# A hand-ordered start for a gated MLP whose up projection uses seven products for eight

## The chip, the cores and the metric

The kernel runs on one core of one Trainium2 chip. The metric is the device time of one execution in microseconds, the median of three runs. The engines are PE (matrix multiply; PEld is its weight load), ACT, DVE and POOL; SP issues the DMA transfers. Activations and weights are float32; for PE each is split into a rounded high part and a low remainder ("fp32r"), and a product is three matmuls: high by high, high by low, low by high.

## The reference

Two layers, 512 tokens, width 1024. Each layer is a token mixer, a cross-attention into 256 memory tokens and a gated MLP, each between an RMS norm before and one after, with a residual sum. The change lies in the MLP (the FFN):

```python
def conv_ffn(h, w_up, conv_w, conv_b, w_down):
    u = causal_dwconv(h @ w_up, conv_w, conv_b)     # width 3
    a, g = jnp.split(u, 2, axis=-1)
    return (jax.nn.gelu(g, approximate=True) * a) @ w_down
```

`w_up` is 1024 x 5632 and `w_down` 2816 x 1024, so the FFN has 22 pairs (j = 0 to 21) of a linear tile and a gate tile, each of 128 features by 512 tokens.

## The kernel before, in words

**Order of the work.** PE always runs in the order in which the program is written. On ACT, DVE, POOL and SP the framework's planner chooses the order, from its own costs and each instruction's dependences, except inside `tc.manual_schedule(engines=...)`: instructions written there keep, on the named engines, the order in which they are written among themselves. Side tasks (the norms) are generators that yield waiting times (the table `PACE`); `drain` runs them to their end, `run` runs a generator and lets side tasks in between.

**Before the FFN.** The output projection of the cross-attention ends tile by tile of 128 tokens (t = 0 to 3). For each, `Tail.consume` adds the residual, and a task `pre_norm` (L241) norms the tile, transposes it on PE (`to_feature`, L272, two halves), writes the high and low parts into `xn` (four B buffers) and copies the float32 values into a piece of the `Forms` object (L283), a T buffer of which there are three. Layer 0 computes four tiles of layer 1's keys (`fill_k`) before its FFN starts.

**The first two pairs.** `ffn` (L1019) computes j = 0 and 1 directly: `feat_halves` (L180) takes the four weight units over the first 256 tokens, calls `between` (here: drain the norm tasks), and takes them over the other 256. As each tile ends, `up_conv` does the convolution (first term on ACT, L1031, the two others on DVE, L1036), the Gelu on ACT (L1058) and the gating product on DVE (L1050). One accumulator bank (`pg`) is held per tile, four in all.

**The other twenty pairs.** `up_products` (L1075) computes each pair j from seven products of 12 matmuls of 256 columns instead of eight: blocks of the input by blocks of the weights, where some operands are sums. The input's sums (s1 to s4) are made by `Forms.add`: four DVE sums for tile 2 with tile 0, four for tile 3 with tile 1 (L310 to L313), and a split of each result (L99 on ACT, L100 on DVE) into the S buffers. The weights' sums (t12, t34) are made by `add_up`, four additions on POOL (L1106 to L1109). `high` (ACT, L1125) and `low` (DVE, L1131; POOL for kind "b") split the weights: "a" plain weights, "t" and "u" sums, "b" a plain half. Products 1, 2, 3 and 4 take the plain input (3 with s4 instead), 5, 6 and 7 take sums. Product 1 goes to a scratch bank (`e1s`, tag `pa`); ACT copies it into the left half of the linear bank (L1170 for j = 2, L1213 later), product 2 adds to that; product 6 adds to the scratch bank, and DVE adds the result of product 5 (copied by ACT, L1190) into the gate bank (L1203), to which product 3 adds; product 7 adds to the scratch bank; ACT copies it to the linear bank's right half (L1178), DVE adds it to the gate bank's (L1179), and product 4 adds to the linear bank's. Since these banks are started by copies, a 512-column matmul first marks each bank as written (in `first`, for j = 2 and 3). PE's order for j = 2 is: two marks, product 1, 5, 6, two marks and product 1 of j = 3, product 2, 3, 7. The hand order on ACT, DVE and POOL is entered just before `up_products`; the first two pairs' work on these engines is left to the planner.

**The down stage.** `down` (L1223) adds 22 steps of eight tiles (h = 1 in four `pa` banks, then h = 0 in four `pg` banks), three matmuls of 512 columns each per tile; steps 0 and 1 are split ahead (`down_tile`). The `pg` banks are those of the last two pairs.

Every matmul has the line L107, every transpose L111.

Of the kernel before, what the change touches and what calls it, by code (L numbers as in the profile page):

```python
# [23 lines left out]
NF = 22  # L24
# [14 lines left out]
def trunk_kernel(ctx: ExitStack, tc: tile.TileContext, x4, memt, w, gw, gains, mcw, fcw, gb,  # L39
# [201 lines left out]
    def pre_norm(t, g, xn, wait, forms=None):  # L241
        xt = xs[t]
        v = None
        xgs = []
        ss = [sumsq(xt[:, 512 * h:512 * h + 512]) for h in range(2)]
        for h in range(2):
            c = slice(512 * h, 512 * h + 512)
            v2 = sm(1, tag="v", bufs=8)
            if h == 0:
                DVE.tensor_scalar(v2, ss[h], 1.0 / D, EPS, ALU.mult, ALU.add)  # L250
            else:
                DVE.scalar_tensor_tensor(v2, ss[h], 1.0 / D, v, ALU.mult, ALU.add)
            v = v2
        r = rstd(v)
        for h in range(2):
            c = slice(512 * h, 512 * h + 512)
            xg = pp.tile([128, 512], F32, tag="xg", name=nm("xg"), bufs=PACE["xg"])
            DVE.scalar_tensor_tensor(xg, xt[:, c], r, g[h], ALU.mult, ALU.mult)  # L258
            xgs.append(xg)
        yield wait  # L260
        while forms and t == 3 and not forms.s:
            yield 0.2
        xf = forms.piece() if forms else None
        for h in range(2):
            to_feature(xgs[h], t, xn[h], xn[2 + h], xf[:, 4 * h:4 * h + 4, :] if forms else None)
            yield PACE["nh"]
        if forms:
            while not forms.free:
                yield 0.2
            forms.add(t, xf)  # L270

    def to_feature(src, t, hi, lo, f32=None):  # L272
        p = pa()
# [9 lines left out]
    class Forms:  # L283


        def __init__(self):
            self.es = ExitStack()
            self.pool = self.es.enter_context(tc.tile_pool(name=nm("forms"), bufs=1, reuse_waits="tile"))
            self.pool.tile([128, 8 * PAD_S], F32, name=nm("pad")) if PAD_S else None
            self.s = None  # L290
            self.free = True
            self.xf = {}

        def wide(self, dt):
            return self.pool.tile([128, 8, 256], dt, tag="S", name=nm("S"), bufs=4)

        def piece(self):
            return self.flat().rearrange("p (k t) -> p k t", k=8)
# [4 lines left out]
        def add(self, t, xf):  # L303
            self.xf[t] = xf
            if t < 2:
                return
            self.s = self.s or [self.wide(F32R) for _ in range(4)]
            a, b = self.xf[t - 2], xf
            a11, a12, a21, a22 = a[:, :4], a[:, 4:], b[:, :4], b[:, 4:]
            DVE.tensor_add(a22, a21, a22)  # L310
            DVE.tensor_sub(a21, a11, a21)
            DVE.tensor_sub(a11, a22, a11)
            DVE.tensor_sub(a12, a12, a11)  # L313
            c = slice(128 * (t - 2), 128 * (t - 2) + 128)
            for i, f in ((0, b), (2, a)):
                split(f, self.s[i][:, :, c], self.s[i + 1][:, :, c])

        def part(self, which):
            i, k = {"s3": (0, 0), "s1": (0, 4), "s2": (2, 0), "s4": (2, 4)}[which]
# [699 lines left out]
    def ffn(l, xn, pend, forms):  # L1019
        act = act_of(xn)  # L1020
        es = ExitStack()
        fp = es.enter_context(tc.tile_pool(name=nm("ffn"), bufs=1, reuse_waits="tile"))
        fcw_t = fp.tile([128, 44, 4], F32, tag="fcw", name=nm("fcw"))
        SP.dma_start(fcw_t, fcw[l])
        gtiles = []
        us = {}

        def conv_first(j, half, acc):
            m = 22 * half + j
            us[j, half] = u = fp.tile([128, 512], F32, tag=f"u{half}", name=nm("u"), bufs=2)  # L1030
            ACT.activation(u, acc, AF.Identity, bias=fcw_t[:, m, 3:4], scale=fcw_t[:, m, 2:3])  # L1031

        def conv_rest(j, half, acc):
            m, u = 22 * half + j, us[j, half]
            for q in range(1, 3):
                DVE.scalar_tensor_tensor(u[:, q:], acc[:, :512 - q], fcw_t[:, m, 2 - q:3 - q], u[:, q:],  # L1036
                                         ALU.mult, ALU.add)

        def gated(j, lin, gate):
            if j < 16:  # L1040
                if j % 4 == 0:
                    us["big"] = bt()
# [10 lines left out]
        def up_conv(j, half, acc):  # L1053
            conv_first(j, half, acc)
            conv_rest(j, half, acc)
            u = us[j, half]
            if half:
                ACT.activation(u, u, AF.Gelu_apprx_tanh)  # L1058
            if (j, 1 - half) in us:
                gated(j, us.pop((j, 0)), us.pop((j, 1)))  # L1060

        def up_done(j, half):
            return lambda acc: up_conv(j, half, acc)

        drain(pend[:2])
        run(feat_halves(l, [U_UP + i for i in range(4)], act, [up_done(i // 2, i % 2) for i in range(4)],
                        lambda: drain(pend)))
        order = ExitStack()
        order.enter_context(tc.manual_schedule(engines={
            mybir.EngineType.Activation, mybir.EngineType.DVE, mybir.EngineType.Pool}))  # L1070
        with tc.manual_schedule(engines={mybir.EngineType.SP}):
            ready = run(up_products(l, fp, xn, forms, us, conv_first, conv_rest, gated, gtiles))
        return es, order, gtiles, ready

    def up_products(l, fp, xn, forms, us, conv_first, conv_rest, gated, gtiles):  # L1075

# [75 lines left out]

        def first(j):
            e1s[j] = pa()[:, left]
            if j < j0 + 2:
                for o in total(j):
                    mm(o, ws[j, "a"][0][:, :128], xn[0][:, 0, :], start=True, stop=True)
            yield from product(e1s[j], j, 1, True)

        for j in (j0, j0 + 1):  # L1160
# [12 lines left out]
        ready = []  # L1173
        for j in range(j0, NF + 1):
            p, real = j - 1, j < NF
# [15 lines left out]
            if p >= j0:  # L1191
                conv_rest(p, 1, G)
                if p > j0:
                    gated(p - 1, us.pop((p - 1, 0)), total(p - 1)[1])
                yield from product(A[:, right], p, 4)
                conv_first(p, 0, A)
                ACT.activation(G, us.pop((p, 1)), AF.Gelu_apprx_tanh)
                conv_rest(p, 0, A)
            if not real:
                gated(p, us.pop((p, 0)), G)  # L1200
                return ready
            yield from product(e1s[j], j, 6)
            DVE.tensor_add(total(j)[1][:, left], e1s[j], p5s[j])  # L1203
            high(j + 1, "t")
            low(j + 1, "t")
            if j + 1 == NF:
                ready.append(down_tile(0))
            else:
                yield from first(j + 1)
            high(j + 2, "a")  # L1210
            low(j + 2, "a")
            if j + 1 < NF:
# [8 lines left out]
            yield from product(e1s[j], j, 7)  # L1221

    def down(l, forms, gtiles, consume, order, ready):  # L1223
        accs = [[pg() for _ in range(4)], [pa() for _ in range(4)]]
        held = []

        def step(k, gh_, gl_, wu, t, h):
# [4 lines left out]
        for k in range(NF):  # L1232
# [8 lines left out]
            if k < NF - HELD:  # L1241
                for h in (1, 0):
                    for t in range(4):
                        step(k, gh_, gl_, wu, t, h)
                        yield
            else:
                order.close()
                held.append((k, gh_, gl_, wu))
# [10 lines left out]
    for l in range(L):  # L1259
# [15 lines left out]
        def cross_done():  # L1275
            drain(tasks)
            es.close()
            tail.open()
            tail.forms.free = l > 0

        run(tok_gen(l, U_WO, act_of([o_t[0], o_t[1], o_t[2], o_t[3]]), (0, 1), tail.consume,
                    seq=early(PACE["ec"], cross_done, lambda u: drain(tasks[u:u + 1]))))
        xn = tail.xn
        if l == 0:
            run(fill_k(mem_tiles(lambda: tail.forms.wide(F32R)), 1, range(PACE["kf"][0])))
            tail.forms.free = True
        pend = tail.tasks
        tail.close()
        forms = tail.forms
# [88 lines left out]
```

## Time and profile before

| | us |
|---|---|
| median of 3 runs | 1570.26 |
| lowest and highest | 1569.21, 1571.17 |
| the profiled execution | 1572.73 |
| its span | 1571.0 |
| PE busy in it | 1546.8 (98%) |
| DVE, ACT, POOL busy | 1049.2, 891.1, 327.6 |
| mean granted clock | 0.998 |

The profile is of one execution. Layer 0's FFN starts about 453 us into the span (its direct tiles), its twenty other pairs run from 476 to 681; in layer 1 these are 1213, and 1238 to 1445. In timelines a row has its start, its length, the engine, the source line, the operation, output<-inputs by names, the shape, and in brackets the engine's idle time before it with what ended it. Instructions of one engine may overlap a little in the records, and matmuls always do, so PE's pace is read from one start to the next.

### The profile page before, as it was taken

The numbers are of one execution on the slowest core, as the hardware profiler recorded it, in microseconds if no ns is written. First come the engines' busy times: TensorE is split into PE (matmuls) and PEld (weight loads), VectorE is DVE, ScalarE is ACT, GpSimd is POOL, SyncE is SP. The second block draws the span as 40 slices with busy tenths as digits, with TensorE's granted clock in tenths as the row PEclk, the third lists the DMA queues.
The fourth block names the chain that finished last, engine by engine and source line by source line (L and its number), as shares of the span: only waits on it lengthen the run. The fifth ranks groups of instructions, "written<-read, shape, count | busy, mean of one in ns | idle before, by whom it ended". The sixth has DMA issues, their size and how long they took to land.

```text
span 1571.0 us, 24501 instructions
## 1 busy us (share of the span) xinstructions
PE 1546.8 (98%) x9480; PEld 1371.6 (87%) x9480; DVE 1049.2 (67%) x1808; ACT 891.1 (57%) x1578; POOL 327.6 (21%) x292
## 2 busy tenths in 40 slices
PE   7999999999999999999999999999999999999998
PEld 5788888997899999988887888889988899999886
DVE  5687656746597777763376876567566977787433
ACT  5677574545466666652256775745445666666321
POOL 0000110100025666600010001101000466663000
PEclk9999999999999999999999999999999999999999
DMA  5331244553242333333323312444511233332321
GB/s 177 129 95 63 92 133 156 159 172 106 68 137 95 108 108 104 100 121 103 111 88 114 95 62 90 135 156 155 165 63 46 93 106 108 108 118 81 126 104 55
DMA packets 55430, 173.13 MB, mean 110 GB/s; under 512 B 6801, under 2 KB 9617, under 8 KB 55314
## 3 DMA queue, kind: packets, MB, share of 16 engines
q1 hardware_dynamic: 55314, 171.57, 33.5%
q8 instruction: 74, 1.21, 0.3%
q14 instruction: 42, 0.34, 0.1%
HBM read 165.22 MB, written 6.33 MB: 109 GB/s over the span
## 4 chain that ended last, share of the span: by engine, by line
PE 82%; DVE 6%; DMA 4%; ACT 3%; issue 2%; POOL 2%; SPq 0%; POOLq 0%; DVEq 0%; ACTq 0%
PE pg L107 51%; PE pa L107 28%; DMA raw<-in_w_dram 3%; PE pa L111 3%; DVE wlo L100 1%; ACT whi L99 1%; DVE xg L258 1%; POOL sm L232 1%; ACT junk L237 1%; DVE x L371 1%; DMA raw<-in_memt_dram 1%; DVE wlo L1131 1%; DVE B L279 0%; DMA raw<-dv 0%; DVE S L100 0%
## 5 line engine op out<-in xcount | busy, mean ns | idle before, releaser
L107 PE MATMUL pg<-B,whi 128*128 128x256 f32 (+1 forms) x1800 | 420.4, 327 | 4.0 <-DVE u L1036 2.5
L100 DVE TENSOR_TENSOR wlo<-raw,whi 128x1024 fp32r<-128x1024 f32 x188 | 231.2, 1231 | 216.6 <-ACT whi L99 216.0
L99 ACT CAST whi<-raw 128x1024 fp32r<-128x1024 f32 x188 | 197.2, 1050 | 221.7 <-PE pg L107 140.1
L107 PEld LDWEIGHTS pg<-B,whi 128*128 128x128 f32 x1800 | 290.2, 189 | 23.2 <-ACT b L1125 2.3
L107 PE MATMUL pg<-whi,B 128*128 128x512 f32 x896 | 297.7, 399 | 0.0
L107 PE MATMUL pg<-B,wlo 128*128 128x256 f32 (+1 forms) x896 | 288.0, 321 | 0.0
L107 PEld LDWEIGHTS pg<-whi,B 128*128 128x128 f32 x896 | 168.5, 188 | 34.9 <-DVE B L100 1.3
L232 POOL TENSOR_TENSOR sm<-sm,mhalf 128x1 f32<-128x1 f32 x56 | 34.3, 612 | 719.9 <-DVE sm L357 543.9
L107 PEld LDWEIGHTS pg<-B,wlo 128*128 128x128 f32 x896 | 168.9, 189 | 13.5
L107 PE MATMUL pg<-wlo,B 128*128 128x512 f32 x448 | 175.3, 391 | 0.6 <-DVE sm L250 0.6
L107 PE MATMUL pa<-S,whi 128*128 128x256 f32 x960 | 175.5, 283 | 0.0
L1036 DVE SCALAR_TENSOR_TENSOR u<-pg,fcw,u 128x511 f32<-128x511 f32 (+1 forms) x176 | 131.4, 747 | 38.2 <-ACT u L1031 35.2
L107 PEld LDWEIGHTS pa<-S,whi 128*128 128x128 f32 x960 | 147.5, 189 | 0.0
L107 PE MATMUL pa<-S,wlo 128*128 128x256 f32 x480 | 135.2, 282 | 0.0
L1131 DVE TENSOR_TENSOR wlo<-T,whi 128x1024 fp32r<-128x1024 f32 x80 | 104.0, 1301 | 10.8 <-ACT whi L1125 10.8
L107 PE MATMUL pa<-whi,S 128*128 128x512 f32 x320 | 105.9, 390 | 0.0
L107 PE MATMUL pg<-whi,S 128*128 128x512 f32 x320 | 105.4, 390 | 0.0
L1125 ACT CAST whi<-T 128x1024 fp32r<-128x1024 f32 x80 | 83.5, 1044 | 33.7 <-PE pg L107 28.6
L1031 ACT ACTIVATE u<-pg,fcw 128x512 f32<-128x512 f32 x88 | 68.5, 778 | 57.8 <-PE pg L107 37.8
L107 PEld LDWEIGHTS pg<-wlo,B 128*128 128x128 f32 x448 | 84.7, 189 | 15.8 <-DVE wlo L100 1.0
L107 PEld LDWEIGHTS pa<-S,wlo 128*128 128x128 f32 x480 | 90.9, 189 | 0.0
L1131 POOL TENSOR_TENSOR b<-rg,b 128x512 fp32r<-128x512 f32 x40 | 51.8, 1294 | 144.2 <-ACT b L1125 144.2
(264 smaller groups left out, 2947.8 us busy)
## 6 DMA issues: line engine op xcount, KB each, us to landing
raw<-in_w_dram SPq DMA_DIRECT2D x228, 512.0 KB, 3.5
rg<-in_w_dram SPq DMA_DIRECT2D x40, 512.0 KB, 3.4
gain<-in_gains_dram SPq DMA_DIRECT2D x11, 512.0 KB, 4.4
raw<-in_memt_dram SPq DMA_DIRECT2D x20, 256.0 KB, 3.1
tb<-tb_d SPq DMA_DIRECT2D x16, 256.0 KB, 3.6
x<-in_x_dram SPq DMA_DIRECT2D x8, 256.0 KB, 5.5
e<-nmu_d SPq DMA_DIRECT2D x8, 256.0 KB, 3.7
dv<-vf SPq DMA_DIRECT2D x8, 256.0 KB, 4.0
```

The source lines that it names most:

```text
L99: ACT.copy(hi, src)
L100: DVE.tensor_sub(lo, src, hi.bitcast(F32))
L107: PE.matmul(o, lhs, rhs, **kw)
L111: PE.transpose(o, src, idn)
L232: POOL.tensor_tensor(r, v, mhalf[:, :1], ALU.pow)
L237: ACT.activation(junk[:, :src.shape[-1]], src, AF.Square, accum_out=s_)
L258: DVE.scalar_tensor_tensor(xg, xt[:, c], r, g[h], ALU.mult, ALU.mult)
L371: DVE.scalar_tensor_tensor(xs[t][:, cc], self.hg[hh, t], r, xs[t][:, cc], ALU.mult, ALU.add)
L1031: ACT.activation(u, acc, AF.Identity, bias=fcw_t[:, m, 3:4], scale=fcw_t[:, m, 2:3])
L1036: DVE.scalar_tensor_tensor(u[:, q:], acc[:, :512 - q], fcw_t[:, m, 2 - q:3 - q], u[:, q:], ALU.mult, ALU.add)
L1125: ACT.copy(ws[j, kind][0], source(j, kind))
L1131: sub(ws[j, kind][1], source(j, kind), ws[j, kind][0].bitcast(F32), ALU.subtract)
```

## The change

- `pre_norm` no longer waits for buffers; tile 3's piece is a B buffer (`late`), which the linear-by-gate products of j = 12 to 15 use later. `Forms.add` is cut into `sums(t, i)` (two DVE sums) and `halve(t, i)` (one split).
- The hand order of ACT, DVE, POOL and of SP's loads is entered in `between`, before the second half of the first two pairs. `up_products` then runs in five steps: one in `between`, one behind each of the four direct tiles. Convolutions, Gelus and gating of j = 0 and 1 stand in that order.
- PE's order for the first products becomes: product 1 of j = 2, mark, product 1 of j = 3, mark, product 2 of j = 2, then 5, 6, mark, product 2 of j = 3, 3, 7. The other mark of j = 3 stands before its product 6.
- At the end, the first tile of down step 0 (three matmuls, h = 1, t = 0) goes before product 4 of the last pair.

```diff
@@ pre_norm
-        while forms and t == 3 and not forms.s:
-            yield 0.2
-        xf = forms.piece() if forms else None
+        xf = forms.piece(t) if forms else None
...
-        if forms:
-            while not forms.free:
-                yield 0.2
-            forms.add(t, xf)
+        if forms and t == 2:
+            forms.sums(t, 0)
@@ Forms
+        def sums(self, t, i):
+            a, b = self.xf[t - 2], self.xf[t]
+            a11, a12, a21, a22 = a[:, :4], a[:, 4:], b[:, :4], b[:, 4:]
+            if i == 0:
+                DVE.tensor_add(a22, a21, a22)
+                DVE.tensor_sub(a21, a11, a21)
+            else:
+                DVE.tensor_sub(a11, a22, a11)
+                DVE.tensor_sub(a12, a12, a11)
+
+        def halve(self, t, i):
             self.s = self.s or [self.wide(F32R) for _ in range(4)]
...
+            split(self.xf[t - 2 * i], self.s[2 * i][:, :, c], self.s[2 * i + 1][:, :, c])
@@ ffn
+        def gelu(j):
+            ACT.activation(us[j, 1], us[j, 1], AF.Gelu_apprx_tanh)
...
+        def between():
+            drain(pend)
+            order.enter_context(tc.manual_schedule(engines={
+                mybir.EngineType.Activation, mybir.EngineType.DVE, mybir.EngineType.Pool}))
+            loads.enter_context(tc.manual_schedule(engines={mybir.EngineType.SP}))
+            next(up)
 
         def up_done(j, half):
-            return lambda acc: up_conv(j, half, acc)
+            def f(acc):
+                conv_first(j, half, acc)
+                conv_rest(j, half, acc)
+            return f
...
-                        lambda: drain(pend)))
+                        between, 4 * [lambda: next(up)]))
+        ready = run(up)
@@ up_products
-        sums = [pg() for _ in range(4)]
+        sums = []
...
         for j in (j0, j0 + 1):
             load_a(j)
             load_g(j)
+        forms.halve(2, 0)
+        forms.sums(2, 1)
+        high(j0, "a")
+        low(j0, "a")
+        forms.halve(2, 1)
         add_up(j0)
         load_a(j0 + 2)
-        for kind in "atu":
-            high(j0, kind)
-            low(j0, kind)
-        high(j0, "b")
-        yield from first(j0)
-        ACT.copy(total(j0)[0][:, left], e1s[j0])
+        yield
+        forms.sums(3, 0)
+        yield
         high(j0 + 1, "a")
         low(j0 + 1, "a")
+        forms.sums(3, 1)
+        forms.halve(3, 0)
+        forms.halve(3, 1)
+        high(j0, "t")
+        low(j0, "t")
+        gelu(0)
+        yield
+        high(j0, "b")
+        high(j0, "u")
+        low(j0, "u")
+        yield
+        gated(0, us.pop((0, 0)), us.pop((0, 1)))
+        gelu(1)
+        gated(1, us.pop((1, 0)), us.pop((1, 1)))
+        yield
+        banks = [pg() for _ in range(4)]
+        sums += [banks[i] for i in (0, 2, 1, 3)]
+        for j in (j0, j0 + 1):
+            yield from first(j)
+            A, G = total(j)
+            mark(A)
+            ACT.copy(A[:, left], e1s[j])
+        yield from product(total(j0)[0][:, left], j0, 2)
...
+                if not real:
+                    first_down = pa()
+                    gh_, gl_, wu = ready[0]
+                    mm3(first_down, gh_[:, :128], gl_[:, :128], wu[0][:, 512:], wu[1][:, 512:], True, False)
+                    yield
                 yield from product(A[:, right], p, 4)
...
+            if j == j0 + 1:
+                mark(total(j)[1])
             yield from product(e1s[j], j, 6)
+            if j == j0:
+                mark(total(j)[1])
             DVE.tensor_add(total(j)[1][:, left], e1s[j], p5s[j])
...
-            yield from product(total(j)[0][:, left], j, 2)
+            if j == j0:
+                yield from product(total(j + 1)[0][:, left], j + 1, 2)
+            elif j > j0 + 1:
+                yield from product(total(j)[0][:, left], j, 2)
```

## Rows read from the trace of the kernel before

**Rows 1.** The page's busy lines: engine, busy us, share, instructions.
```profile
PE 1546.8 (98%) x9480; PEld 1371.6 (87%) x9480; DVE 1049.2 (67%) x1808; ACT 891.1 (57%) x1578; POOL 327.6 (21%) x292
```
**Rows 2.** The chain of waits, layer 0's FFN: start, length, engine and line, count.
```profile
484.92 2.88 PE pg L107 x24
```
**Rows 3.** PE's timeline where layer 0's other pairs begin.
```profile
476.07 0.40 PE L107 MATMUL pg<-B,whi 128*128 128x512 f32 x1
477.00 0.48 PE L107 MATMUL pg<-B,whi 128*128 128x512 f32 x1 [0.53 <-DVE u L1036]
...
482.05 0.40 PE L107 MATMUL pa<-B,whi 128*128 128x256 f32 x2
483.45 0.39 PE L107 MATMUL pa<-B,wlo 128*128 128x256 f32 x1 [1.00 <-DVE wlo L1131]
```
**Rows 4.** PE's timeline where layer 1's other pairs begin.
```profile
1238.14 0.47 PE L107 MATMUL pg<-B,whi 128*128 128x512 f32 x1
1240.59 0.77 PE L107 MATMUL pg<-B,whi 128*128 128x512 f32 x1 [1.98 <-DVE u L1036]
1241.16 0.63 PE L107 MATMUL pa<-B,whi 128*128 128x256 f32 x2
...
1243.72 0.49 PE L107 MATMUL pa<-S,whi 128*128 128x256 f32 x2
...
1247.38 0.39 PE L107 MATMUL pa<-B,whi 128*128 128x256 f32 x2
1249.04 0.39 PE L107 MATMUL pa<-B,wlo 128*128 128x256 f32 x1 [1.26 <-DVE wlo L1131]
```
**Rows 5.** Windows: stretch, length, PE, PEld, DVE, ACT, POOL busy, granted clock, DMA.
```profile
1240.50:1243.90 3.40, 3.31 (x14) 3.24 (x15) 3.10 (x3) 2.84 (x4) 3.32 (x3) 0.50 0.61 212
...
1226.00:1238.00 12.00, 11.57 (x96) 11.18 (x94) 11.90 (x13) 6.62 (x8) 6.32 (x4) 1.00 0.01 2
```
**Rows 6.** PE's timeline between product 7 and product 4 of layer 0's last pair.
```profile
679.19 0.28 PE L107 MATMUL pa<-S,wlo 128*128 128x256 f32 x1
679.91 0.50 PE L107 MATMUL pg<-B,whi 128*128 128x256 f32 x2 [0.45 <-ACT pg L1178]
```
**Rows 7.** ACT's timeline, layer 0: table load, copy for j = 2, second Gelu.
```profile
476.93 1.28 ACT L1058 ACT_TABLE_LOAD   x1 [0.92 <-DVE u L1036]
...
479.43 0.37 ACT L1170 COPY pg<-pa 128x256 f32<-128x256 f32 x1
...
481.42 0.63 ACT L1058 ACTIVATE u<-u 128x512 f32<-128x512 f32 x1 [0.65 <-DVE u L1036]
```
**Rows 8.** Groups by shape, ACT, 484 to 660: count, busy us, mean ns, idle before.
```profile
L1125 ACT CAST whi<-T 128x1024 fp32r<-128x1024 f32 x35 | 36.6, 1045 | 14.8 <-PE pg L107 14.8
L1031 ACT ACTIVATE u<-pg,fcw 128x512 f32<-128x512 f32 x34 | 26.5, 778 | 25.2 <-PE pg L107 16.7 <-DVE pg L1179 8.5
...
L1213 ACT COPY pg<-pa 128x256 f32<-128x256 f32 x18 | 6.6, 369 | 0.7 <-PE pa L107 0.7
```
**Rows 9.** Groups by shape, DVE, 484 to 660.
```profile
L1036 DVE SCALAR_TENSOR_TENSOR u<-pg,fcw,u 128x511 f32<-128x511 f32 x34 | 25.4, 747 | 14.9 <-ACT u L1031 14.9
L1131 DVE TENSOR_TENSOR wlo<-raw,whi 128x1024 fp32r<-128x1024 f32 x18 | 21.8, 1212 | 0.0
```
**Rows 10.** DVE's and POOL's timelines, layer 0: one kind of sum twice, an addition.
```profile
453.60 0.69 DVE L311 TENSOR_TENSOR T<-T,T 128x512 f32<-128x512 f32 x1
...
463.20 1.68 DVE L311 TENSOR_TENSOR T<-T,T 128x512 f32<-128x512 f32 x1
...
461.61 2.72 POOL L1106 TENSOR_TENSOR T<-rg,raw 128x512 f32<-128x512 f32 x1 [14.66 <-DVE B L279]
```
**Rows 11.** DVE's timeline, layer 1: the last scaling before tile 3's transposes.
```profile
1220.42 1.42 DVE L258 SCALAR_TENSOR_TENSOR xg<-x,sm,gain 128x512 f32<-128x512 f32 x2
```
**Rows 12.** DVE's timeline, layer 0: the last pair's convolution and gating.
```profile
683.22 1.53 DVE L1036 SCALAR_TENSOR_TENSOR u<-pg,fcw,u 128x511 f32<-128x511 f32 x2
...
684.85 0.69 DVE L1050 TENSOR_TENSOR gt<-u,pg 128x512 f32<-128x512 f32 x1
```

More of the change, by code (lines that the diff above doesn't have):

```diff
@@ L290, in __init__, with piece @@
             self.s = None
-            self.free = True
             self.xf = {}
+            self.late = None
         def wide(self, dt):
             return self.pool.tile([128, 8, 256], dt, tag="S", name=nm("S"), bufs=4)
-        def piece(self):
-            return self.flat().rearrange("p (k t) -> p k t", k=8)
+        def piece(self, t):
+            if t == 3:
+                self.late = bt()
+            f = self.late.rearrange("p a b -> p (a b)")[:, :1024] if t == 3 else self.flat()
+            self.xf[t] = f.rearrange("p (k t) -> p k t", k=8)
+            return self.xf[t]
         def flat(self, dt=F32):
             return self.pool.tile([128, 1024], dt, tag="T", name=nm("T"), bufs=3)
[L303 to L306, printed above, removed]
-            self.s = self.s or [self.wide(F32R) for _ in range(4)]
[L308 to L313, printed above, removed]
+        def sums(self, t, i):
[8 more added lines that the diff above has]
+        def halve(self, t, i):
+            self.s = self.s or [self.wide(F32R) for _ in range(4)]
             c = slice(128 * (t - 2), 128 * (t - 2) + 128)
-            for i, f in ((0, b), (2, a)):
-                split(f, self.s[i][:, :, c], self.s[i + 1][:, :, c])
+            split(self.xf[t - 2 * i], self.s[2 * i][:, :, c], self.s[2 * i + 1][:, :, c])
         def part(self, which):
@@ L1041, in gated @@
                 if j % 4 == 0:
-                    us["big"] = bt()
+                    us["big"] = bt() if j < 12 else forms.late
                 gt = us["big"][:, j % 4, :]
@@ L1051, in gated, with up_products @@
             gtiles.append(gt)
[L1053 to L1060, printed above, removed]
+        def gelu(j):
+            ACT.activation(us[j, 1], us[j, 1], AF.Gelu_apprx_tanh)
+        order, loads = ExitStack(), ExitStack()
+        up = up_products(l, fp, xn, forms, us, conv_first, conv_rest, gelu, gated, gtiles)
+        def between():
[4 more added lines that the diff above has]
+            next(up)
         def up_done(j, half):
-            return lambda acc: up_conv(j, half, acc)
+            def f(acc):
+                conv_first(j, half, acc)
+                conv_rest(j, half, acc)
+            return f
         drain(pend[:2])
         run(feat_halves(l, [U_UP + i for i in range(4)], act, [up_done(i // 2, i % 2) for i in range(4)],
-                        lambda: drain(pend)))
[L1068 to L1072, printed above, removed]
+                        between, 4 * [lambda: next(up)]))
+        ready = run(up)
+        loads.close()
         return es, order, gtiles, ready
-    def up_products(l, fp, xn, forms, us, conv_first, conv_rest, gated, gtiles):
+    def up_products(l, fp, xn, forms, us, conv_first, conv_rest, gelu, gated, gtiles):
         j0 = 2
@@ L1154, in first, with mark @@
             e1s[j] = pa()[:, left]
-            if j < j0 + 2:
-                for o in total(j):
-                    mm(o, ws[j, "a"][0][:, :128], xn[0][:, 0, :], start=True, stop=True)
             yield from product(e1s[j], j, 1, True)
+        def mark(o):
+            mm(o, ws[j0, "a"][0][:, :128], xn[0][:, 0, :], start=True, stop=True)
         for j in (j0, j0 + 1):
@@ L1200, in up_products @@
                 gated(p, us.pop((p, 0)), G)
-                return ready
+                return ready, first_down
+            if j == j0 + 1:
+                mark(total(j)[1])
             yield from product(e1s[j], j, 6)
+            if j == j0:
+                mark(total(j)[1])
             DVE.tensor_add(total(j)[1][:, left], e1s[j], p5s[j])
@@ L1207, in up_products @@
                 ready.append(down_tile(0))
-            else:
+            elif j > j0:
                 yield from first(j + 1)
@@ L1211, in up_products @@
             low(j + 2, "a")
-            if j + 1 < NF:
+            if j0 < j < NF - 1:
                 ACT.copy(total(j + 1)[0][:, left], e1s[j + 1])
-            yield from product(total(j)[0][:, left], j, 2)
+            if j == j0:
+                yield from product(total(j + 1)[0][:, left], j + 1, 2)
+            elif j > j0 + 1:
+                yield from product(total(j)[0][:, left], j, 2)
             high(j + 1, "u")
@@ L1223, in down @@
     def down(l, forms, gtiles, consume, order, ready):
-        accs = [[pg() for _ in range(4)], [pa() for _ in range(4)]]
+        ready, first_down = ready
+        accs = [[pg() for _ in range(4)], [first_down] + [pa() for _ in range(3)]]
         held = []
@@ L1243, in down @@
                     for t in range(4):
-                        step(k, gh_, gl_, wu, t, h)
-                        yield
+                        if k or t or not h:
+                            step(k, gh_, gl_, wu, t, h)
+                            yield
             else:
@@ L1278, in cross_done @@
             tail.open()
-            tail.forms.free = l > 0
         run(tok_gen(l, U_WO, act_of([o_t[0], o_t[1], o_t[2], o_t[3]]), (0, 1), tail.consume,
@@ L1285, in trunk_kernel @@
             run(fill_k(mem_tiles(lambda: tail.forms.wide(F32R)), 1, range(PACE["kf"][0])))
-            tail.forms.free = True
         pend = tail.tasks
```

## The prediction

> **What bounds the kernel now.** I read the page's busy lines first: PE is busy 98% of the span [rows 1], so a change that leaves the number of matmuls alone can win or lose only where PE stands still. The chain of waits then gives PE's pace in the FFN: 24 matmuls of 256 columns in 2.88 us, 0.12 us each [rows 2]; one of 512 columns I count at 0.23, twice the columns. With that pace I went along PE's timeline around each FFN's start and end and took what is above it as lost. In layer 0 the second mark starts 0.93 after the first, 0.70 more than its 0.23, released by a DVE convolution; and the low part of j = 3's first weights comes 1.40 after two matmuls worth 0.24, a loss of 1.16 [rows 3]. Sum 1.86. In layer 1 the same places cost 2.45 - 0.23 = 2.22, then 0.57 - 0.23 = 0.34, then 1.66 - 0.24 = 1.42 [rows 4], sum 3.98. There the clock falls as well: the granted clock is 0.50, the 1.2 GHz level, in 1240.5 to 1243.9 [rows 5], and the 12 matmuls from 1241.16 take 2.56 instead of 1.44, a loss of 1.12 [rows 4]. Layer 1's start costs 5.1 in all. At the end of the up products PE stands 0.60 (0.72 less 0.12) until ACT has copied a left-hand sum [rows 6]; this stop stands once in each layer. Everything in reach is 1.86 + 5.1 + 1.2 = 8.2 us.
>
> The windows say why the start stalls: DVE is busy 11.90 of the 12.00 us in which the second half of layer 1's first four tiles runs [rows 5]. It is late with sums, splits and convolutions, and PE waits at whichever result it needs first.
>
> **Part by part.**
>
> *What is not changed in amount.* Seven products of 12 matmuls per j, four marks, eight sums, the splits: all the same number. Two products (first of j = 3, second of j = 2) go ahead of product 5. Until product 2 of j = 2 begins, PE now has two products and two marks, 24 x 0.12 + 2 x 0.23 = 3.34 us, that need no sum. `piece(3)` takes a B buffer in place of a T, and the up products later use it as their fourth big tile: no instruction more, nothing. The T buffers of tiles 0 and 2 come free before tile 3's sums, so POOL's four additions for j = 2 go earlier; PE waits for none of them today, nothing.
>
> *What the hand order puts in a row.* The order on ACT and DVE now begins before the second half of the first four tiles and holds the convolutions, both Gelus and the gating, which the planner placed freely. Product 2 of j = 2 adds onto a bank that ACT must first fill by its copy; the copy is written behind `gelu(1)`, and that needs the last direct tile's convolution. Today the copy runs ahead of that Gelu (479.43 against 481.42) [rows 7]. So PE, 3.34 us after its last direct tile, waits for this chain, counted from the end of the second direct tile, (0,1):
>
> first convolution term on ACT 0.78, the two others on DVE 2 x 0.75, low part of j = 3's "a" 1.21, sums(3,1) 2 x 0.69; cast of the last half 1.05, cast "t" 1.05, table load 1.28, Gelu 0.63, ACT term of tile (1,0) 0.78, DVE 2 x 0.75, low "u" 1.21, DVE 2 x 0.75 for tile (1,1), Gelu 0.63, copy 0.37 [rows 7 to 10]. That is 14.9; two DVE instructions of 0.75 span 1.42 [rows 9, 11], so neighbours on one engine overlap by 0.08, some 0.4 in the chain: 14.5. Up to the sums it is 4.8, behind them 9.7.
>
> *Layer 0.* The last direct tile ends at 476.07 [rows 3], so tile (0,1) ends 48 x 0.12 = 5.76 earlier, at 470.3. The copy is through at 484.8; PE arrives at 476.07 + 3.34 = 479.4. New stall 5.4, old 1.86: +3.5. A DVE with nothing else to do cannot shorten this, since sums(3,0) and sums(3,1) now stand behind the convolutions. Bounds, with 14.0 and 15.2 for the chain: +3.0 and +4.2.
>
> *Layer 1.* PE arrives at 1238.14 + 3.34 = 1241.5. By the chain from the end of tile (0,1), 1232.4 + 14.5, the copy is there at 1246.9. By DVE's load: it is free at 1221.84 [rows 11]; up to sums(3,1) stand eight sums and two feature splits of 0.69, four operations of 1.21 and four convolution terms of 0.75, 14.7, less 18 x 0.08: 1235.1. POOL's four additions fall into this, and a sum took 1.68 instead of 0.69 while POOL was adding [rows 10]; four such are 4.0, none is 0, I take the middle, 2: 1237.1 + 9.7 = 1246.8. Both say 1247, with 1246.5 and 1249 as bounds. New stall 5.5 (5.0 to 7.5), old 3.98: +1.5.
>
> *The clock.* A stop of 2.45 was followed by the 1.2 GHz level in layer 1 [rows 4, 5]; those of 0.93 and 1.40 in layer 0 cost the following matmuls nothing, which keep 0.12 [rows 2, 3]. Stops of 5.4 and 5.5 should bring it in both. I price each at the 1.1 that the rows show, between 0 and three times that: layer 0 +1.1, layer 1 1.1 - 1.1 = 0.
>
> *The three down matmuls.* 3 x 0.23 = 0.68 fills the stop of 0.60: product 4 begins at 679.19 + 0.12 + 0.68 = 679.99 [rows 6], as before, ends at 681.43, and the down stage starts 0.68 ahead. Five of its tiles later, at 684.83, PE reaches the bank of A(21), one more on, at 685.51, that of G(21); DVE frees them at 684.75 and 685.54 [rows 12], plus some 0.1 of handing over: 0.15 is given back. Gain 0.55 per layer (0 to 0.7): -1.1.
>
> *j = 3's product 3* follows its product 6 by 12 matmuls instead of 24, 1.44 us for a DVE add that stands behind a convolution. Counted from product 4's end the add is through after 0.78 + 1.42 + 0.42 and two handings over, about 3.0, and product 3 arrives at 0.23 + 24 x 0.12 = 3.1: nothing, at worst 0.3.
>
> Sum: layer 0 +3.5 + 1.1, layer 1 +1.5 + 0, down -1.1: **+5.0 us**. The profiled execution took 1572.73 (span 1571.0), 2.5 above the median 1570.26; the difference is carried over to the median: 1575.3.
>
> On the step that decides, the trace shows ACT idle 14.8 us in all before 35 "whi<-T" casts that wait for PE, with later work queued behind them [rows 8]; that nothing ever passes it does not prove. The Trainium skill, "TensorE: Matmul & The Clock Gate" (Architectural detail: the array is 16x 32x32), says that the queues of ACT and DVE are strictly first in, first out. By it the copy cannot pass a waiting Gelu, and the two stalls stand; were it not so, rival A would hold.
>
> **The rivals.**
>
> *A, faster: the copy is not late.* If the copy is taken before `gelu(1)`, 3.34 us of new cover meet the old waits: 1.86 in layer 0 and 5.1 in layer 1 go, and the down gain comes on top: -8.1, 1562.2. For it: low "t" and the halves, which product 5 needs, are ready three DVE operations after sums(3,1), at about 478.7 and 1240.8, just when PE would arrive. Against: rows 7 show the free order only because the planner placed the Gelu. It decides at a copy done by 479.4 and 1241.5.
>
> *B, no change: the chain holds, but the clock stays up* in both layers: 3.5 + 1.5 - 1.1 (layer 1's old loss) - 1.1 = +2.8, and +1.9 with the lower bounds of the stalls: 1572.2 to 1573.1. For: layer 0's stops cost no clock. Against: 5.4 is over twice the stop that did.
>
> *C, much slower: the hand order starts late.* If in layer 0 DVE does not take tile 0's and 2's halves while the first half runs, 11 of its 13 us before sums(3,1)'s end begin only at 476.07 - 96 x 0.12 = 464.5: 464.5 + 11 + 2 + 9.7 = 487.2, 2.4 later; with the clock's upper bound, 2.2 more in each layer, 1577.7 to 1582.1. For: all these operations are written behind `between`. Against: DVE ran layer 0's sums(2) at 453.6, well ahead of that point [rows 10].
>
> **How the numbers follow.** Forecast 60%, A 14%, B 16%, C 10%. The forecast's own range: stalls -1.0 to +2.7, clock up to +4.4, down +1.1 around +5.0; the ends rarely meet, so 1573 to 1579.5. The whole range leaves out most of A and C's upper end: 1567.0 to 1580.5. A difference under 0.2%, 3.1 us, cannot be told from no change here. The forecast is slower by more than that in about nine of ten, C always, the lower half of B and a tenth of the forecast are no change: slower 0.68, same 0.18, faster 0.14.
>
> **What would show it.** PE's timeline has one long stop in each FFN's start, between a mark and a "pg<-B" matmul of 256 columns, released by ACT's copy that fills the bank; ahead of it ACT's rows run table load, Gelu, term, two casts, term, Gelu, copy. Its length, 5.4 and 5.5, tests the chain; a granted clock of 0.50 behind it in both layers, with matmuls of 0.21, tests the price. The 0.60 stop before product 4 is gone. No long stop, or a copy ahead of the second Gelu, would make the forecast wrong.

## The result and the profile after

The changed kernel takes 1580.35 us (median; 1579.50 to 1581.21) against 1570.72 of the kernel before in the same comparison, a ratio of 1.0063 with a 95% interval of 1.0050 to 1.0076: slower by 9.6. I had forecast slower by 5.0, and no more than 1580.5. The profiled execution took 1581.21, span 1579.4. PE's work is what it was [rows 1]:

```profile
PE 1547.1 (98%) x9480; PEld 1371.6 (87%) x9480; DVE 1052.8 (67%) x1808; ACT 892.2 (56%) x1578; POOL 331.2 (21%) x292
```

I numbered the matmuls of both traces and subtracted the start of the n-th before from the n-th after. The difference is -0.3 ahead of layer 0's other pairs, +5.8 once they have begun, +3.95 at their end, +3.4 after the first down products; +9.0 once layer 1's pairs have begun, +8.5 at the end (1581.21 - 1572.73). So four places matter: the two starts (+6.15, +5.5), layer 0's pairs (-1.9), the down stages (-0.5 each).

PE's timeline after, layer 0's start, where [rows 3] had two short stops:

```profile
478.82 0.39 PE L107 MATMUL pg<-B,whi 128*128 128x512 f32 x1
485.13 0.80 PE L107 MATMUL pg<-B,whi 128*128 128x256 f32 x2 [5.91 <-ACT pg L1200]
485.72 0.41 PE L107 MATMUL pg<-B,wlo 128*128 128x256 f32 x1
485.94 0.63 PE L107 MATMUL pg<-B,whi 128*128 128x256 f32 x2
```

and layer 1's, where [rows 4] had three:

```profile
1244.09 0.40 PE L107 MATMUL pg<-B,whi 128*128 128x512 f32 x1
1253.52 0.79 PE L107 MATMUL pg<-B,whi 128*128 128x256 f32 x2 [9.02 <-ACT pg L1200]
```

One stop in each layer: 6.31 - 0.23 = 6.08 and 9.43 - 0.23 = 9.20 us. Both stand between the second mark and product 2 of j = 2 and end with ACT's copy into the bank, L1200. Behind each the clock is at the 1.2 GHz level; windows of that stretch, columns as in [rows 5]:

```profile
483.30:490.10 6.80, 4.97 (x23) 4.97 (x24) 4.06 (x3) 1.17 (x3) 5.15 (x4) 0.50 0.23 73
1247.90:1258.10 10.20, 4.58 (x21) 4.59 (x22) 7.58 (x7) 3.49 (x7) 8.16 (x5) 0.50 0.20 56
```

PE is busy only from the end of the stop on: 23 matmuls in 4.97 instead of 23 x 0.119 = 2.74, 21 in 4.58 instead of 2.50. The price is 2.2 and 2.1. Before, the clock fell in layer 1 alone, 1.12 by [rows 4]; e7 shows that this cost nothing in the end.

ACT's timeline after, layer 0, is the chain of the forecast in its order, against [rows 7]:

```profile
475.08 1.05 ACT L99 CAST S<-T 128x1024 fp32r<-128x1024 f32 x1 [2.18 <-DVE T L311]
476.04 1.04 ACT L1129 CAST whi<-T 128x1024 fp32r<-128x1024 f32 x1
477.10 1.28 ACT L1054 ACT_TABLE_LOAD   x1
478.40 0.63 ACT L1054 ACTIVATE u<-u 128x512 f32<-128x512 f32 x1
...
481.05 0.78 ACT L1031 ACTIVATE u<-pg,fcw 128x512 f32<-128x512 f32 x1
484.18 0.63 ACT L1054 ACTIVATE u<-u 128x512 f32<-128x512 f32 x1 [2.35 <-DVE u L1036]
484.71 0.63 ACT L1200 COPY pg<-pa 128x256 f32<-128x256 f32 x2
```

ACT is idle for 2.35 in front of the second Gelu while both copies, whose products ended by 479.1, wait behind it.

DVE's timeline after, layer 1, with POOL's beside it; compare the pairs of rows in [rows 10]:

```profile
1227.74 1.23 DVE L100 TENSOR_TENSOR S<-T,S 128x1024 fp32r<-128x1024 f32 x1 [1.11 <-ACT S L99]
...
1230.68 1.56 DVE L311 TENSOR_TENSOR T<-T 128x512 f32<-128x512 f32 x1
1232.16 2.33 DVE L1135 TENSOR_TENSOR wlo<-raw,whi 128x1024 fp32r<-128x1024 f32 x1
...
1235.55 1.52 DVE L1036 SCALAR_TENSOR_TENSOR u<-pg,fcw,u 128x511 f32<-128x511 f32 x2
1236.99 1.83 DVE L307 TENSOR_TENSOR B<-B 128x512 f32<-128x512 f32 x1
...
1242.76 0.69 DVE L311 TENSOR_TENSOR T<-T 128x512 f32<-128x512 f32 x1
```

```profile
1230.38 1.31 POOL L1110 TENSOR_TENSOR T<-rg,raw 128x512 f32<-128x512 f32 x1 [6.54 <-ACT B L277]
1231.77 1.63 POOL L1111 TENSOR_TENSOR T<-rg,T 128x512 f32<-128x512 f32 x1
1235.71 1.32 POOL L1112 TENSOR_TENSOR T<-rg 128x512 f32<-128x512 f32 x1 [2.30 <-DVE S L100]
1236.99 1.29 POOL L1113 TENSOR_TENSOR T<-raw,T 128x512 f32<-128x512 f32 x1
```

Three DVE instructions beside POOL's additions are stretched: 1.56 for 0.69, 2.33 for 1.21, 1.83 for 0.69, together 3.1. The convolution terms at 1235.55, which read a `pg` bank, run beside the third addition in their usual 1.52. The Trainium skill, "SBUF — State Buffer" (Who interferes with whom), says that a DVE instruction with two inputs in SBUF contends with a GpSimd (POOL) instruction that reads SBUF, and that one with at most one such input, outside DVE's 2-port modes, does not; these rows agree. Such stretches stand in the kernel before as well: in layer 1, at 1229.61, 1231.32 and 1235.44, DVE took 1.68, 1.68 and 1.90 for 0.69, 0.69 and 1.22. So the contention is not new with the change. sums(3,1), the last row of the first fence, ends at 1243.45.

The three down matmuls stand in the old stop of [rows 6]; PE's timeline after:

```profile
683.27 0.40 PE L107 MATMUL pa<-whi,T 128*128 128x512 f32 x1
683.50 0.40 PE L107 MATMUL pa<-wlo,T 128*128 128x512 f32 x1
683.74 0.39 PE L107 MATMUL pa<-whi,T 128*128 128x512 f32 x1
683.97 0.42 PE L107 MATMUL pg<-B,whi 128*128 128x256 f32 x2
```

### The profile page after: what moved, and what is told of

The parts are those of the page before. It is cut to its first block, busy times and chain, and to the rows that moved or that the text cites. A ratio compares the mean times of both kernels' runs of the same rounds, so it can differ in the third digit from the quotient of the medians.

```text
span 1579.4 us, 24488 instructions
## 1 busy us (share of the span) xinstructions
PE 1547.1 (98%) x9480; PEld 1371.6 (87%) x9480; DVE 1052.8 (67%) x1808; ACT 892.2 (56%) x1578; POOL 331.2 (21%) x292
## 3 DMA queue, kind: packets, MB, share of 16 engines
q8 instruction: 74, 1.21, 0.3%
HBM read 165.22 MB, written 6.33 MB: 109 GB/s over the span
## 5 line engine op out<-in xcount | busy, mean ns | idle before, releaser
L107 PE MATMUL pg<-B,whi 128*128 128x256 f32 (+1 forms) x1800 | 421.1, 327 | 15.0 <-ACT pg L1200 14.9
L1135 DVE TENSOR_TENSOR wlo<-T,whi 128x1024 fp32r<-128x1024 f32 x80 | 107.8, 1347 | 5.0 <-ACT whi L1129 5.0
L1135 POOL TENSOR_TENSOR b<-rg,b 128x512 fp32r<-128x512 f32 x40 | 55.4, 1385 | 155.0 <-ACT b L1129 155.0
```

Of the source, the lines that this page charges most:

```text
L107: PE.matmul(o, lhs, rhs, **kw)
L1135: sub(ws[j, kind][1], source(j, kind), ws[j, kind][0].bitcast(F32), ALU.subtract)
```

## Experiments

The theory: the stops come from the place of the two copies in ACT's hand order. The rivals: the new order of PE's products itself; the load on DVE and POOL; the clock; something in the other pairs. Each version is the changed kernel with one edit, unless said otherwise. A ratio is to the kernel before in the same comparison; its median lay between 1569.92 and 1571.01 there, so differences of about 1 between versions say nothing.

For some versions I also give the length of the two starts in the trace: from the first matmul of the second half of the first four tiles to the 346th behind it, idle ones not counted. It is 49.90 and 53.55 in the changed kernel (layers 0 and 1), 43.83 and 48.05 in the first execution of the kernel before, 43.73 and 48.39 in e7.

**e1: the second Gelu and the gating behind the copies.**

```diff
-        gated(0, us.pop((0, 0)), us.pop((0, 1)))
-        gelu(1)
-        gated(1, us.pop((1, 0)), us.pop((1, 1)))
...
             ACT.copy(A[:, left], e1s[j])
+        gated(0, us.pop((0, 0)), us.pop((0, 1)))
+        gelu(1)
+        gated(1, us.pop((1, 0)), us.pop((1, 1)))
```

> One edit of the changed kernel: gating of j = 0, the second Gelu and gating of j = 1 are written behind ACT's two bank copies instead of ahead of them. Theory 1 (the stop is ACT's copy standing in the chain behind the second Gelu): the copy now stands directly behind the last direct tile's ACT term, which in the changed kernel ran at 481.05 and 1249.44; it is through about 1.2 later, so PE goes on near 482.4 and 1250.8, the stops are 3.3 and 6.5 instead of 6.1 and 9.2, with a fall of the clock behind each as now; about 5.4 us less than the changed kernel, near 1575. Theory 2 (DVE's backlog holds PE wherever the copy stands: PE would stop as long at product 5): no gain, within 1 us of 1580.4.

Measured: 1574.07, ratio 1.0026 (1.0014 to 1.0037). PE's timeline, the ends of the two stops:

```profile
481.23 0.51 PE L107 MATMUL pg<-B,whi 128*128 128x256 f32 x2 [2.95 <-ACT pg L1197]
...
1245.46 0.79 PE L107 MATMUL pg<-B,whi 128*128 128x256 f32 x2 [5.94 <-ACT pg L1197]
```

The stops are 3.11 and 6.10, shorter by 3.0 and 3.1, and in this execution the clock falls in layer 1 alone; one new stop of 0.66 comes before product 3 of j = 3. The place of three lines is worth 1580.35 - 1574.07 = 6.3. The rest of the loss, over 3 us, stays; in ACT's timeline the copies now run right behind the last direct tile's term (480.13 and 480.80 in layer 0).

**e2: PE's new order kept, the hand order entered only behind the four direct tiles** (as before; the planner places the convolutions, Gelus and gating).

```diff
         def between():
             drain(pend)
-            order.enter_context(tc.manual_schedule(engines={
...
-            loads.enter_context(tc.manual_schedule(engines={mybir.EngineType.SP}))
             next(up)
...
+        order.enter_context(tc.manual_schedule(engines={
...
+        loads.enter_context(tc.manual_schedule(engines={mybir.EngineType.SP}))
         ready = run(up)
```

> The changed kernel's matmul order, its buffers and the down matmuls, but the hand order is entered only behind the four direct tiles, as in the kernel before; the planner orders ACT, DVE and POOL until then. Theory 1 (the hand order costs, PE's new order is free or gains): ACT copies the banks ahead of the second Gelu, the long stops go, and what is left are short waits for product 5's operands: at or under the kernel before, 1562 to 1571. Theory 2 (PE's new order itself costs, since product 2 needs a copy that product 5 did not): stops of 3 us or more stay before product 2, and the time stays over 1573.

Measured: 1569.65, ratio 0.9991 (0.9981 to 1.0002). ACT's timeline, layer 0:

```profile
478.73 0.63 ACT L1054 ACTIVATE u<-u 128x512 f32<-128x512 f32 x1
479.27 0.76 ACT L1031 ACTIVATE u<-pg,fcw 128x512 f32<-128x512 f32 x1
479.93 0.37 ACT L1200 COPY pg<-pa 128x256 f32<-128x256 f32 x1
483.21 0.63 ACT L1054 ACTIVATE u<-u 128x512 f32<-128x512 f32 x1 [2.91 <-DVE u L1036]
```

The first copy runs ahead of the second Gelu, as in [rows 7]; PE's stops before product 2 are 2.00 and 2.63, and the clock falls behind both. So the loss comes with the early hand order (of SP's loads too). PE's new order, together with the down matmuls, can't be told from the kernel before in time. In the trace it is no gain either: the starts take 45.13 and 48.47, 1.4 and 0.1 more than in e7, and each down stage gives back 0.5.

**e3: the kernel before with the three down matmuls moved** (in `up_products`, before product 4 of the last pair; `down` skips that tile).

```diff
+                if not real:
+                    first_down = pa()
+                    gh_, gl_, wu = ready[0]
+                    mm3(first_down, gh_[:, :128], gl_[:, :128], wu[0][:, 512:], wu[1][:, 512:], True, False)
+                    yield
```

> The kernel before with the first tile of down step 0 moved before product 4 of the last pair, and nothing else. Theory 1: the 0.60 stop before product 4 is filled in each layer and some 0.5 of it is kept: 1.0 us less than the kernel before (1569.7), with a trace in which PE is 0.5 ahead behind each FFN's end. Rival: the bank of the linear half is freed too late and all of it is given back: 0. For the second question, PE's pace of 0.1200 in layer 0's pairs before against 0.1187 in the changed kernel: if it belongs to the program's buffers, layer 0's pairs here run at 0.1200 as before.

Measured: 1570.00, ratio 0.9999 (0.9989 to 1.0008). The 0.6 stops are gone; in time a gain of 1 can't be told from none here.

**e4: idle matmuls in the stops**, 46 in layer 0, 72 in layer 1, into a scratch bank, so that PE does not stand.

```diff
+        idle = pa()
+        for _ in range((46, 72)[l]):
+            mm(idle[:, left], ws[j0, "a"][0][:, :128], xn[0][:, 0, left], start=True, stop=True)
         yield from product(total(j0)[0][:, left], j0, 2)
```

> The changed kernel with matmuls that need nothing and whose result is not used, 46 of 256 columns in layer 0 and 72 in layer 1, ahead of product 2 of j = 2, where PE stands 6.1 and 9.2 us. ACT's copy is as late as before; PE is busy until 0.6 us ahead of it. Theory 1 (the clock's fall behind each stop costs PE some 2.4 us per layer): the granted clock stays at 1.00 through both starts and the time is 4.5 to 5 us under the changed kernel's, 1575.5. Rival (behind the stop PE is held by DVE and ACT anyway): the clock stays up and the time does not change by 1 us. On the pace: if layer 0's faster pace in the changed kernel, 0.1187 against 0.1200, comes with the fall of the clock, its pairs run at 0.1200 here and 1.9 us of the gain are missing (1577.4).

Measured: 1576.11, ratio 1.0040 (1.0025 to 1.0055). The windows around the ends of the stops, as long as those of the changed kernel above:

```profile
483.50:490.30 6.80, 6.74 (x56) 6.70 (x57) 4.22 (x5) 3.22 (x6) 3.50 (x3) 1.00 0.24 78
1249.70:1259.90 10.20, 10.20 (x85) 10.15 (x86) 6.54 (x7) 4.87 (x8) 5.29 (x5) 1.00 0.18 54
```

The clock stays up and product 2 begins as long after the mark as it did (6.33 against 6.31 in layer 0): 1580.35 - 1576.11 = 4.2 is the price of the clock alone. The starts in the trace say the same, 47.71 and 51.55: 2.2 and 2.0 less.

**e5: without POOL's four additions for j = 2**; that pair's sums of weights are left out, and its t and u weights are values that are there already.

```diff
-            if j < NF:
+            if j == j0:
+                ts[j] = [forms.xf[t].rearrange("p k t -> p (k t)") for t in (0, 2)]
+            elif j < NF:
```

> The changed kernel without POOL's four additions for j = 2: its "t" and "u" are split from the float32 pieces of tiles 0 and 2 instead, so pair j = 2 is computed from other data; all else stands. Theory 1 (in layer 1 DVE's own backlog, stretched by POOL's additions, moves the chain): three of DVE's operations that took 1.56, 2.33 and 1.83 there take 0.69, 1.21 and 0.69, DVE is through sums(3,1) 3 us earlier, and layer 1's stop goes from 9.2 to 6.5 +- 0.5 (the chain from the second direct tile's end, 15.0 in layer 0, lets no more than 3.3 go); layer 0's stays at 6.1. Rival (handing over between ACT and DVE sets both stops): 9.2 stays within 1.

Measured, one run: 1577.45. PE's timeline at the ends of the two stops, then DVE's, the three instructions of layer 1 that POOL had stretched:

```profile
484.03 0.80 PE L107 MATMUL pg<-B,whi 128*128 128x256 f32 x2 [5.91 <-ACT pg L1202]
...
1249.77 0.79 PE L107 MATMUL pg<-B,whi 128*128 128x256 f32 x2 [5.97 <-ACT pg L1202]
```

```profile
1229.99 0.68 DVE L311 TENSOR_TENSOR T<-T 128x512 f32<-128x512 f32 x1
1230.59 1.22 DVE L1137 TENSOR_TENSOR wlo<-raw,whi 128x1024 fp32r<-128x1024 f32 x1
...
1234.38 0.68 DVE L307 TENSOR_TENSOR B<-B 128x512 f32<-128x512 f32 x1
```

Layer 0's stop is unchanged (6.07), layer 1's is 6.14 instead of 9.20: the 3.1 that layer 1 loses more than layer 0 is POOL's additions stretching DVE.

**e6: all of the Gelus, the gating and the splits of "b" and "u" behind the copies**.

```diff
-        gelu(0)
...
-        high(j0, "b")
-        high(j0, "u")
-        low(j0, "u")
...
-        gated(0, us.pop((0, 0)), us.pop((0, 1)))
-        gelu(1)
-        gated(1, us.pop((1, 0)), us.pop((1, 1)))
...
             ACT.copy(A[:, left], e1s[j])
+        gelu(0)
+        high(j0, "b")
+        high(j0, "u")
+        low(j0, "u")
+        gated(0, us.pop((0, 0)), us.pop((0, 1)))
+        gelu(1)
+        gated(1, us.pop((1, 0)), us.pop((1, 1)))
```

> The changed kernel with all that the two bank copies do not need written behind them: both Gelus, the splits "b" and "u" of j = 2, and the gating. ACT then has "t" of j = 2, the two direct tiles' terms, the copies. Theory 1: in layer 0 the copy is through at 478.9, when PE arrives (479.05): a stop under 0.3. In layer 1 it is 1.8 behind the "t" cast's end: a stop near 3.1 instead of 9.2, with a clock fall (2 us). 12 us and layer 0's 2.2 for the clock less than the changed kernel: 1566 +- 1.5, under both kernels. Rival (product 5 and what follows wait for the "u" split and the table load that now come later): stops of 3 us turn up behind product 2, and the time is over 1570.

Measured: 1573.89, ratio 1.0027 (1.0011 to 1.0043); 1566 was missed, and the rival's condition held. PE's timeline, its long waits:

```profile
487.51 2.93 PE L107 MATMUL pg<-S,b 128*128 128x256 f32 x12 [3.18 <-DVE pg L1241]
...
1243.40 0.51 PE L107 MATMUL pg<-B,whi 128*128 128x256 f32 x2 [2.70 <-ACT pg L1193]
...
1252.35 1.86 PE L107 MATMUL pg<-S,b 128*128 128x256 f32 x7 [2.75 <-DVE pg L1241]
```

The copy's stop is gone in layer 0 and 2.86 in layer 1, but product 3 now waits 3.34 and 2.91 for the DVE add into the gate bank. DVE's timeline, layer 0:

```profile
482.27 1.47 DVE L1135 TENSOR_TENSOR wlo<-T,whi 128x1024 fp32r<-128x1024 f32 x1 [1.69 <-ACT whi L1129]
483.66 3.45 DVE L1050 TENSOR_TENSOR B<-u,u 128x512 f32<-128x512 f32 x2
487.04 0.42 DVE L1241 TENSOR_TENSOR pg<-pa,p 128x256 f32<-128x256 f32 x1
```

The add stands behind both gating products, which take 3.45 while POOL adds.

**e7: the kernel before once more**, unchanged.

> The kernel before, unchanged, profiled once more. In its first profile PE's pace in layer 0's twenty pairs was 0.1200 us per matmul, in every other kernel's and in layer 1 0.1187. If the pace changes from one execution to the next, it may be 0.1187 here, with the span 1.9 us shorter (1569); if it belongs to the program, it is 0.1200 again and the span 1571.

Measured, one run: 1569.24, span 1567.5, 3.5 less than the first profiled execution. Windows of 520 to 620 in layer 0's pairs, where PE never stands; first that of the first profiled execution of the kernel before:

```profile
520.00:620.00 100.00, 100.00 (x836) 100.00 (x835) 78.69 (x100) 64.94 (x99) 63.25 (x51) 1.00 0.32 106
```

that of this execution:

```profile
520.00:620.00 100.00, 100.00 (x845) 100.00 (x844) 78.89 (x101) 65.59 (x101) 64.02 (x51) 1.00 0.33 107
```

and that of the changed kernel:

```profile
520.00:620.00 100.00, 100.00 (x845) 100.00 (x845) 80.29 (x102) 65.58 (x102) 65.61 (x52) 1.00 0.32 106
```

The execution on which I had built got 836 matmuls into these 100 us, 0.120 each, the two others 845, less than 0.119 each, all with a granted clock of 1.00. In e3 and e4 these pairs ran at the faster pace too. That is the -1.9 in layer 0's pairs, and it belongs to the execution, not to the change. In this one PE stood 2.22 in layer 1's start, as in [rows 4], and the clock did not fall: 1.00 in 1237.0 to 1240.5. PE's timeline, the marks of j = 3 and the low part of its weights:

```profile
1241.78 0.39 PE L107 MATMUL pg<-B,whi 128*128 128x512 f32 x1
1243.65 0.47 PE L107 MATMUL pg<-B,whi 128*128 128x512 f32 x1 [1.48 <-DVE u L1036]
...
1245.59 0.39 PE L107 MATMUL pa<-B,wlo 128*128 128x256 f32 x1 [1.23 <-DVE wlo L1131]
```

PE came to the marks sooner and stood 1.87 - 0.23 = 1.64 for DVE there. From the first mark (1234.70) to the row of 1245.59 it took 10.89; in the first execution, with the clock down, 1249.04 - 1238.14 = 10.90 [rows 4]. The slow matmuls there ran in time in which PE would have waited for DVE.

**e8: e6 with both Gelus and the gating behind the DVE add of j = 2.**

```diff
             DVE.tensor_add(total(j)[1][:, left], e1s[j], p5s[j])
+            if j == j0:
+                gelu(0)
+                gelu(1)
+                gated(0, us.pop((0, 0)), us.pop((0, 1)))
+                gated(1, us.pop((1, 0)), us.pop((1, 1)))
```

> As in the version with the copies ahead of the Gelus, but both Gelus and the gating of tiles 0 and 1 now stand behind the DVE add of j = 2's product 4, so that nothing of them is ahead of any result that PE waits for in the start. Theory (what costs is the place of the copies and adds in the order of ACT and DVE): both stops before product 3 of j = 2 go (3.34 and 2.91 there), layer 0 has no stop over 1, layer 1 keeps the copy's stop of about 2.9 and perhaps a clock fall of up to 2; against the version before it 3.3 + 2.9 + some 2 of clock less: 1573.9 - 7.5 = about 1566, below the kernel before by 3 to 5. Rival (the FFN's start holds more work on ACT and DVE than the time there, wherever it stands): the stops only move on, to j = 2's product 7 or to j = 4's first up tiles, and the time stays at 1570 to 1574.

Measured: 1573.76, ratio 1.0018 (1.0009 to 1.0027). 1566 was missed. As the rival said, the stops only moved on and the time stayed, though the places are others than it named. PE's timeline, its long waits in layer 0:

```profile
489.81 0.38 PE L107 MATMUL pa<-S,wlo 128*128 128x256 f32 x1 [1.46 <-DVE wlo L1135]
...
497.68 1.81 PE L107 MATMUL pg<-S,b 128*128 128x256 f32 x12 [1.89 <-DVE pg L1237]
```

No stop is left before product 3 of j = 2. Now product 5 of j = 3 waits for the low part of its t weights, and product 3 of j = 3 for its add, both on DVE. Layer 1 keeps the copy's 2.84 and has the same two (1.09, 2.09). In layer 0 the stops sum to 3.7, against 1.86 before the change. In none of the three orders (e1, e6, e8) was DVE's work of the start in time.

**e9: e2 with 14 and 19 idle matmuls in its stops.**

```diff
+        idle = pa()
+        for _ in range((14, 19)[l]):
+            mm(idle[:, left], ws[j0, "a"][0][:, :128], xn[0][:, 0, left], start=True, stop=True)
```

> The version in which the hand order begins only behind the four direct tiles (2.00 and 2.63 of stop before product 2 of j = 2, then 14 matmuls at 0.213 in each layer), with 14 matmuls (layer 0) and 19 (layer 1) into an unused bank in that stop. Theory (the clock falls because PE stands, and costs 14 x (0.213 - 0.119) = 1.3 in each layer; the rest of the new order is worth what the stops say): the clock stays up in both starts, 2.6 off 1569.65: about 1567, a ratio near 0.998 to the kernel before. Rival (the clock's fall is put off or falls elsewhere, or the idle matmuls are themselves in the way of the copy): no gain, 1569 to 1571.

Measured: 1569.08, ratio 0.9994 (0.9985 to 1.0003). The clock stayed at 1.00 in both starts, and these take 43.65 and 47.55 in the trace, 1.5 and 0.9 less than in e2: 2.4 of the 2.6 forecast. In time 1567 was missed. The profiled execution (1571.91) ran layer 1's pairs at the slower pace, so its span can't show the gain:

```profile
1300.00:1400.00 100.00, 100.00 (x835) 100.00 (x835) 78.33 (x100) 65.19 (x100) 64.15 (x50) 1.00 0.33 106
```

In time neither this nor e2 can be told from the kernel before, and no version that I ran is shown to beat it.

## Why the prediction was right in kind and short in size

*The mechanism* was right and is shown: one long stop in each layer, at the place and with the releaser forecast; the earlier copy in e2 removes most of it, and moving three lines in e1 takes 3.0 and 3.1 off. By the traces layer 0 cost +6.15 against +4.6 forecast (stall and clock), layer 1 +5.5 against +1.5, the down matmuls -1.0 against -1.1. On the order of ACT's queue, the rule that I had weighed from the Trainium skill, "TensorE: Matmul & The Clock Gate" (Architectural detail: the array is 16x 32x32), that ACT works strictly first in, first out, agrees with the row of 484.18: ACT idles 2.35 with ready copies queued behind.

*Layer 0's stall*, forecast 5.4, was 6.08. The last direct tile ended 0.3 sooner than in the trace of before, and so did PE's arrival; the chain took 14.9 instead of 14.5, from 470.24 to 485.13. That is the bare sum of its rows: the 0.4 of overlap that I took off was used up by the handing over from engine to engine. I had also read it from the wrong pair: the 1.42 of [rows 11] is of L258, while two convolution terms span 1.53 [rows 12]. A further 0.2 went from PE to ACT: the last direct tile ended at 475.74, so tile (0,1) at 475.74 - 48 x 0.119 = 470.03, and ACT began on it at 470.24.

*Layer 1's stall is the step that failed in size*: forecast 5.5, bounds to 7.5, measured 9.20. With e5 it splits: 6.1 is the chain as in layer 0, 3.1 is POOL. I had priced POOL's additions at 2, and then found that the chain from tile (0,1) gave the same 1247, so that they cost nothing in the forecast. But the additions run while DVE is on its way to sums(3,1), and these decided: they were through at 1243.45, against 1237.1 + 3.4 (the shift of the trace by then) = 1240.5, 2.9 late. Of that POOL is 1.1 (3.1 for the 2 priced); 1.1 is DVE standing for ACT's cast (the row of 1227.74), which I had put at nothing; the last 0.7 is overlap between DVE's neighbours, of which I had taken off 18 x 0.08 = 1.4 and the rows from 1225.22 to 1243.45 give 0.75. The copy was through at 1253.5 - 3.4 = 1250.1 on the clock of the forecast, 1.1 behind my outer bound of 1249. PE also arrived 0.6 sooner, as two small waits of 0.9 in the direct tiles shrank to 0.3.

*The clock* was mis-sized: 1.1 a layer from one row, measured 2.1 (e4). My upper bound of three times held it. In [rows 4] 12 slow matmuls followed the stop; behind those of 6 and 9 there are 23 and 21. A price read behind a short stop did not carry over to a long one, and by e7 the 1.1 was not even a price: PE would have waited in that time with the clock up.

*The base*: the profiled execution of before was 1.9 slow in layer 0's pairs through its pace, and I carried its 2.5 above the median over as a constant. By the traces the terms of the change are 6.15 + 5.5 - 1.0 = 10.7, against 5.0. In the difference of the two profiled executions, 8.5, the pace hides 1.9 of that; the medians, 9.6 apart, lie in between.

*The down matmuls*: forecast -0.55 a layer, by the traces -0.5. *Product 3 of j = 3*: waits of 0.14 and 0.22, within the 0.3.

*The rivals.* A fell: the copies came last. B fell: the clock dropped in both layers. C's time, 1577.7 to 1582.1, holds the result, but not its mechanism: in layer 0 DVE had stood idle 5.34 us before tile (0,0)'s convolution at 468.21, so the halves of tiles 0 and 2 were not late. DVE's timeline after:

```profile
468.21 1.53 DVE L1036 SCALAR_TENSOR_TENSOR u<-pg,fcw,u 128x511 f32<-128x511 f32 x2 [5.34 <-ACT u L1031]
```

## What to carry to other kernels

When a hand order takes over work that a planner had placed, look for the cheapest instruction that PE needs (here a copy of 0.37) and for what is written ahead of it: taking one late Gelu and the gating from ahead of it won 3 us in each stop, 6.3 in all. Moving the late work further back won no more here: e6 and e8 only moved the stops from the copy to the add to the split. Where two bounds of a stall agree by chance, price the contention anyway, since it moves whichever of the two ends up later.

## What I had not expected of the hardware

- PE's pace through a stage without any wait has two values, 0.1187 and 0.120 us for 256 columns, at a granted clock of 1.00; it holds for a stage (layer 0's pairs in the first execution of before, layer 1's in e9) and changes between executions. What sets it stays open.
- The clock falls after some stops of 2 to 3 us and not after others. After 2.22 it fell in the first execution of before and not in e7; it fell after 2.22 in e3, 2.00 and 2.63 in e2, 3.34 and 2.91 before product 3 in e6 and the last stop of 2.1 in each layer of e8, and not after 3.11 in layer 0 of e1, 2.86 in layer 1 of e6 or 2.84 in layer 1 of e8. After each of the stops of 6 and 9 that I saw, it fell.
- Two gating products of 0.69 on DVE took 3.45 while POOL added (e6): two and a half times as long.
